# A two-layer encoder trunk on one core: the seams between a down projection and the next up projection reordered, six pairs begun in them instead of four

## The chip, the cores and the metric

The kernel runs on one core of one Trainium2 chip, as one launch. The metric is the device time of an execution in microseconds (us). The engines are called PE (matrix products and transposes), ACT (activations, copies, also a DMA queue), DVE (vector operations) and SP (a DMA queue); a thing "on PE" is an instruction in that engine's own queue.

## What is computed

The reference is a trunk of two layers over x of 1024 rows (tokens) by 1024 columns. Layer 0 mixes by a short gated convolution, layer 1 by attention over shared keys and values. Both are followed by a squared-ReLU MLP, and each of these four blocks is wrapped in the same way:

```python
h = modulate(rmsnorm(x, norm_g[l, 0]), sh_m, sc_m)
y = short_conv_mixer(h, ...) if l < N_A else mla_mixer(h, ...)
x = x + g_m[:, None, :] * rmsnorm(y, norm_g[l, 1])
h = modulate(rmsnorm(x, norm_g[l, 2]), sh_f, sc_f)
y = jnp.square(jax.nn.relu(h @ mlp_up_w[l])) @ mlp_down_w[l]
x = x + g_f[:, None, :] * rmsnorm(y, norm_g[l, 3])
```

So at the end of every block a product y is complete row by row, y is normalised and added to x, x is normalised again, scaled and shifted, and the result h is what the next block's first product takes. Between the two products lie two norms, a transposition and a split, for all 1024 rows. That stretch is called a seam here.

## The kernel before

**Numbers.** Every f32 factor is split into a high and a low part ("split": ACT writes the high part, DVE subtracts it for the low part; `split_w`, line 162), and a product is three matmuls (`mm`, line 158). One matmul is 128 by 128 by 512.

**Pairs.** The up projections (`mlp_up`, line 1051, and `all_pairs`, line 480) take the weight columns in pairs of 128, 16 pairs, and compute a pair against both halves of h (512 rows each) with seven instead of eight block products, in the manner of Strassen and Winograd. The operands on the side of h are quarters called "11", "21", "22" and the sums t1 to t4. "11" and "21" need only the first half of h (rows 0 to 511, y tiles 0 to 3); the others need the second half too. A product (`prod`, line 472) is twelve matmuls. A pair is "begun" when its products with "11" and "21" have been made ahead; the other five follow later. `AHEAD` (line 36) says how many pairs are begun in the seam. For a begun pair the later sums are taken by DVE (line 513), for the others by copies on ACT (line 511) and further adds.

**The seam** is written out by hand in the class `Seam` (line 258). The last round of the down projection (`down`, line 742) computes y in eight tiles of 128 rows; each is 24 matmuls in one of two wide PSUM tiles ("big"). After each tile t, `Seam.tile` (line 288) does this:

- DVE adds the tile from PSUM to y[t] (line 299);
- `back` (line 278) runs the splits left over from the last turn;
- `squares` (line 242): ACT squares y[t], sums the row and takes the root;
- `flush` (line 282): ACT normalises the tile before, y[t-1] <- x[t-1] times the reciprocal root (line 285);
- from t = 5 on, `front` (line 272) runs two steps of the first half: per step four transposes of y[0..3] on PE into a "tp" PSUM tile, of which there are two, and one eviction on ACT with scale and shift (lines 360 and 361; in the seam of layer 0's MLP lines 420 and 422). Its back, two operations on DVE (371 and 372, or 426 and 427), makes the split;
- DVE scales y[t] by its root and gain gmb (line 305) and adds it to x (line 306); the ACT queue stores x; ACT squares x[t], which the next flush uses.

Eight steps make the first half (`steps0`): six in tiles 5 to 7, the last two behind the seam's first product.

**Order.** `pinned` (line 101) chains every instruction issued in its block to the one before on the same engine, for all engines but SP. Inside such a block the order on an engine is the order of the program. Instructions outside, such as the matmuls of the next tile, are placed by the compiler's scheduler, which can put them ahead of a pinned instruction that it takes to be not ready.

**After the last tile** there are two forms. Seams one and three (behind the convolution's and the attention's output product) go to `first_pairs` (line 576): first(i) is the product of pair i with "11" and a copy of it on ACT (586); second(i) is the product with "21", added to the same PSUM bank, and its ReLU (590). Between them stand the turns of the second half: four steps (`steps1`), each of eight transposes and two evictions into a raw buffer (`front1`, 374) and a back (`back1`, 387) of five splits: five copies on ACT (382), eight subtractions on DVE (385 and 392 to 399). Pair 0's weight sums (`pair_sums`, 456) stand there too, and the five products that need the second half end it. Weights of pairs 0 to 2 are split before the seam; pair 3's come through the buffer "acc". Seam two (behind layer 0's MLP) goes to `first_block` (line 556): eight rounds of nine matmuls, with the second half turned from round 4 on.

**Buffers.** Raw buffers (line 91) are four and hold x tiles, weight blocks and turned quarters; row buffers (line 97) are eight and hold the eight y tiles, later the pairs' results; "acc" and "gmb" (in `ad`) are one each; split weights of a pair half have three.

**The last phase** is layer 1's down projection: the same `tile`, without the second norm, and `finish` (line 314) for its tile 7, in two halves.

Of the kernel before, what the change touches and what calls it, by code (L numbers as in the profile page):

```python
# [8 lines left out]
F32 = mybir.dt.float32  # L9
# [8 lines left out]
P = 128  # L18
D = 1024
# [13 lines left out]
SM = 1.0 / math.sqrt(NOPE + ROPE)  # L33
MASKED = -(2.0 ** 127)
SLOTS = 6
AHEAD = 4
ROWS = 4
LAG = 2
PAIRS = (D_FF // P - ROWS) // 2
# [10 lines left out]
def trunk_kernel(ctx: ExitStack, tc: tile.TileContext, x, c, ada_w, ada_b, norm_g, conv_in_w, conv_w,  # L50
# [31 lines left out]
    def mm_ps():  # L82
        return ps.tile([P, HALF], F32, tag="mm", name=nm("mm"))
# [166 lines left out]
    def rroot(rt):  # L250
        rs = small()
        nc.vector.reciprocal(rs, rt)
        return rs
# [4 lines left out]
    class Seam:  # L258
# [29 lines left out]
        def tile(self, t, p_, steps):  # L288
            y = self.ys[t]
            if t == 0:  # L290
                self.load(0)
                self.load(1)
            self.load(t + 2)
            xr = self.xr[t]
            if self.last and t == NT - 1:
                self.finish(t, y, xr, p_)
                return
            with pinned():
                nc.vector.tensor_tensor(y, y, p_, op=ALU.add)  # L299
                self.back()  # L300
                ss = squares(self.nx, y)
                self.flush()
                if t >= 5:
                    self.front(steps, 2)
                nc.vector.scalar_tensor_tensor(y, y, rroot(ss), self.gmb, op0=ALU.mult, op1=ALU.mult)  # L305
                nc.vector.tensor_tensor(xr, xr, y, op=ALU.add)  # L306
                nc.scalar.dma_start(self.xdst[t * P:(t + 1) * P, :], xr)
                if not self.last:
                    self.rest = (y, xr, squares(self.nx, xr))

        def finish(self, t, y, xr, p_):

# [240 lines left out]
    def first_block(seam, steps0, steps1, ws, h):  # L556

        ps_ = [mm_ps(), mm_ps(), big_ps()[:, :HALF]]
        for k in range(KD):
            with pinned():  # L560
                for p_, w in zip(ps_, ws):
                    mm(p_, (w[0][:, k, :], w[1][:, k, :]), (h[0][:, k, :], h[1][:, k, :]), k == 0, k == KD - 1)
                if k == 0:
                    seam.back()
                    seam.front(steps0, 2)
                    seam.flush()
                elif k == 1:
                    seam.back()
                elif k >= 4:
                    seam.back()  # L570
                    seam.front(steps1, 2)
        with pinned():
            seam.back()
        return ps_

    def first_pairs(seam, steps0, steps1, up, wmat, ws, ops):

        banks(True)
        tiles = [mm_ps(), mm_ps(), bank_ps(), bank_ps()]
        ca = [row_tile() for _ in range(AHEAD)]  # L580
        late = ad.tile([P, D], F32, tag="acc", name=nm("w"), bufs=1).rearrange("p (k m) -> p k m", k=KD)
        ld(late, wmat[:, 2 * (AHEAD - 1) * P:(2 * AHEAD - 1) * P].rearrange("(k p) m -> p k m", p=P))

        def first(i):
            prod(tiles[i], (ws[i], 0, "11"), ops)
            nc.scalar.activation(ca[i][:, HALF:], tiles[i], AF.Copy)  # L586

        def second(i):
            prod(tiles[i], (ws[i], 4, "21"), ops, False)
            nc.scalar.activation(ca[i][:, :HALF], tiles[i], AF.Relu)  # L590

        a, b = load_pair(wmat, 0)
        with pinned():
            first(0)
            seam.back()
            seam.front(steps0, 2)
            first(1)
            seam.back()
            seam.flush()
            second(0)  # L600
            ws.append(up_split(up, late))
            sums = pair_sums(up, a, b)
            next(sums)
            second(1)
            next(sums)
            seam.front(steps1, 1)
            rest = next(sums)
            first(2)
            seam.front(steps1, 1)
            seam.backs.pop(0)()  # L610
            second(2)
            rest.update(next(sums))
            first(3)
            seam.front(steps1, 1)
            seam.backs.pop(0)()
            out_ = {6: mm_ps(), 5: mm_ps(), 3: bank_ps(), 7: bank_ps(), 4: bank_ps()}
            for kk in range(4):
                for j in (5, 6, 4, 3, 7):
                    prod(out_[j], rest[j], ops, kks=[kk])
                if kk == 0:  # L620
                    second(3)
                    seam.front(steps1, 1)
                if kk < 2:
                    seam.backs.pop(0)()
            p1, cb = ca[0][:, HALF:], row_tile()
            c21, c22 = halves(cb)
            nc.vector.tensor_tensor(c21, p1, out_[6], op=ALU.add)
            nc.vector.tensor_tensor(c22, c21, out_[5], op=ALU.add)
            nc.vector.tensor_tensor(c21, c21, out_[4], op=ALU.add)
            nc.vector.tensor_tensor(p1, c22, out_[3], op=ALU.add)  # L630
            nc.vector.tensor_tensor(c22, c22, out_[7], op=ALU.add)
            nc.vector.tensor_tensor(c21, c21, out_[7], op=ALU.add)
# [396 lines left out]
    def down_phase(slots, sizes, wd, src_fn, g, xsrc, xdst, next_w, key, ys=None, pairs=True):  # L1029
# [6 lines left out]
        if pairs:  # L1036
# [1 line left out]
            hs = {n: as_quarter(slots[i]) for n, i in zip(names, (2, 3, 0, 1, 4, 5))}  # L1038
            hs["t4"] = {}
            steps0, steps1 = quarter_steps(ys, key, hs)  # L1040
            wcols = [next_w[:, 2 * i * P:(2 * i + 1) * P] for i in range(AHEAD - 1)]
        else:
            hs = [as_h(slots, H0), as_h(slots, H1)]
            steps0, steps1 = h_steps(tp, ys, 0, key, hs[0]), h_steps(tp, ys, 1, key, hs[1])
# [468 lines left out]
```

## Time and profile before

| | |
|---|---|
| median of 3 timed runs | 2180.91 us (2180.79 to 2181.0) |
| the profiled execution | 2184.31 us |
| its span, first to last instruction | 2182.5 us |
| mean granted clock of PE | 0.992 |
| busy: PE, DVE, ACT | 2091.3, 1518.8, 1065.7 us |
| DVE's add of tile 7, seams one, two, three | 389.86, 1047.39, 1534.77 us |

A line of the timeline gives the start and duration in us, the engine and source line, the operation, output <- input by the program's names, shapes and the count of instructions merged into it; in brackets the idle time of the engine ahead of it and what ended that. `L160` is the helper `mm`, so its lines are told apart by the names of tiles: "one", "mm" and "big" are PSUM tiles, "uphi" and "uplo" split weights, "slot" and "q" the operands made of h. A line of the waits gives the total, the number and the longest.

### The profile page before, as it was taken

Reading aid. Unit: us, or ns where it says so; the run is one execution under the profiler, and the core shown is the slowest. Engines: PE = TensorE matmul, PEld = TensorE weight load, DVE = VectorE, ACT = ScalarE, POOL = GpSimd, SP = SyncE. Lnnn points to the kernel's source line nnn. Section 1 sums busy time; section 2 is a strip of 40 time slices with the busy share of each in tenths; the row PEclk is TensorE's granted clock in tenths of the full one; section 3 lists DMA queues with packets and bytes.
Section 4 is the critical chain, followed back from the end, with each engine's and each line's share of the span. In section 5 each row is a group of like instructions: output and inputs, shape, how many; then the busy total and the mean of one; then the engine's idle time right before and its main releaser. Section 6 shows DMA issues by size and latency. Waiting matters only on the chain.

```text
span 2182.5 us, 25285 instructions
## 1 busy us (share of the span) xinstructions
PE 2091.3 (96%) x9654; PEld 1716.8 (79%) x9654; DVE 1518.8 (70%) x2009; ACT 1065.7 (49%) x1515; POOL 4.0 (0%) x8
## 2 busy tenths in 40 slices
PE   4999999899999999999899999999899999999998
PEld 3788878678888778888777888878678888788887
DVE  6877776876665578956788776665866665458556
ACT  4533354744454433344665555564744454444342
POOL 0000000000000000000000000000000000000000
PEclk9999999999999999999999999999999999999999
DMA  7444463256543987445224231053245553853243
GB/s 225 125 133 141 137 211 134 78 164 212 169 159 107 323 273 262 155 146 173 86 65 121 70 113 44 25 163 122 77 158 185 184 179 113 312 199 129 97 145 135
DMA packets 240255, 329.90 MB, mean 151 GB/s; under 512 B 18597, under 2 KB 141826, under 8 KB 240134
## 3 DMA queue, kind: packets, MB, share of 16 engines
q1 hardware_dynamic: 202248, 247.52, 36.2%
q10 hardware_dynamic: 37886, 80.77, 9.8%
q8 instruction: 76, 1.25, 0.2%
q14 instruction: 45, 0.37, 0.1%
HBM read 247.50 MB, written 80.74 MB: 150 GB/s over the span
## 4 chain that ended last, share of the span: by engine, by line
PE 73%; DVE 13%; ACT 6%; DMA 5%; issue 2%; ACTq 0%; SPq 0%; DVEq 0%
PE one L160 37%; PE mm L160 19%; PE tp L160 7%; PE big L160 4%; DMA raw<-in_ada_w_dram 3%; PE big L1306 2%; ACT junk L245 2%; DVE y L305 2%; DVE raw L306 2%; DVE acc L185 1%; PE tp L1332 1%; DVE y L299 1%; DVE av L847 1%; DMA raw<-ha 1%; DVE small L1309 1%
## 5 line engine op out<-in xcount | busy, mean ns | idle before, releaser
L160 PE MATMUL one<-slot,uphi 128*128 128x512 f32 x1224 | 377.8, 390 | 0.0
L160 PE MATMUL big<-slot 128*128 128x512 f32 x1152 | 268.0, 392 | 1.0 <-ACT y L770 0.6
L160 PEld LDWEIGHTS one<-slot,uphi 128*128 128x128 f32 x1224 | 230.6, 188 | 48.1 <-issue 0.5
L160 PEld LDWEIGHTS big<-slot 128*128 128x128 f32 x1152 | 216.0, 188 | 46.7 <-ACT y L770 1.4
L164 DVE TENSOR_TENSOR uplo<-raw,uphi 128x1024 fp32r<-128x1024 f32 x127 | 153.0, 1221 | 137.1 <-ACT uphi L163 137.1
L160 PE MATMUL one<-slot,uplo 128*128 128x512 f32 x612 | 240.8, 393 | 6.7 <-ACT y L586 2.3
L160 PE MATMUL one<-ring,ring 128*128 128x512 f32 x1008 | 232.3, 391 | 6.5 <-DVE ring L164 6.5
L163 ACT ACTIVATE ring<-w 128x1024 fp32r<-128x1024 f32 x98 | 103.8, 1059 | 261.4 <-PE tp L160 131.6
L160 PEld LDWEIGHTS one<-ring,ring 128*128 128x128 f32 x1008 | 188.2, 188 | 49.4 <-ACT ring L163 5.5
L163 ACT ACTIVATE uphi<-raw 128x1024 fp32r<-128x1024 f32 x127 | 134.5, 1061 | 129.5 <-PE one L160 89.1
L164 DVE TENSOR_TENSOR ring<-w,ring 128x1024 fp32r<-128x1024 f32 x98 | 119.8, 1222 | 107.5 <-ACT ring L163 107.4
L160 PE MATMUL mm<-slot,uphi 128*128 128x512 f32 x520 | 165.0, 398 | 9.7 <-DVE slot L385 9.3
L160 PE MATMUL mm<-ring,ring 128*128 128x512 f32 x672 | 162.4, 390 | 0.0
L160 PE MATMUL tp<-ring,ring 128*128 128x512 f32 x672 | 161.8, 389 | 0.0
L185 DVE SCALAR_TENSOR_TENSOR acc<-raw,csil,acc 128x1024 f32<-128x1024 f32 x88 | 112.8, 1282 | 49.8 <-DMA raw<-in_ada_w_dram 47.6
L160 PEld LDWEIGHTS mm<-ring,ring 128*128 128x128 f32 x672 | 125.7, 188 | 27.1 <-DVE ring L164 0.6
L160 PEld LDWEIGHTS tp<-ring,ring 128*128 128x128 f32 x672 | 126.2, 188 | 26.2
L160 PEld LDWEIGHTS one<-slot,uplo 128*128 128x128 f32 x612 | 115.3, 188 | 34.2 <-ACT y L511 3.3
L164 DVE TENSOR_TENSOR ring<-raw,ring 128x1024 fp32r<-128x1024 f32 x98 | 119.5, 1219 | 18.1 <-ACT ring L163 18.1
L160 PEld LDWEIGHTS mm<-slot,uphi 128*128 128x128 f32 x520 | 97.7, 190 | 33.2 <-DVE slot L385 10.8
L511 ACT ACTIVATE y<-one 128x512 f32<-128x512 f32 x66 | 39.0, 591 | 170.7 <-PE one L160 83.8
L160 PE MATMUL one<-slot,s 128*128 128x512 f32 x468 | 114.2, 393 | 0.7 <-DVE s L164 0.7
(262 smaller groups left out, 3473.3 us busy)
## 6 DMA issues: line engine op xcount, KB each, us to landing
ha<-y ACTq DMA_DIRECT2D x196, 256.0 KB, 3.9
raw<-ha SPq DMA_DIRECT2D x98, 512.0 KB, 4.0
raw<-in_ada_w_dram SPq DMA_DIRECT2D x80, 512.0 KB, 4.4
raw<-in_mlp_up_w_dram SPq DMA_DIRECT2D x70, 512.0 KB, 4.3
w<-in_mlp_down_w_dram SPq DMA_DIRECT2D x56, 512.0 KB, 5.9
raw<-hd SPq DMA_DIRECT2D x24, 512.0 KB, 4.5
xs<-raw ACTq DMA_DIRECT2D x24, 512.0 KB, 3.1
raw<-xs SPq DMA_DIRECT2D x24, 512.0 KB, 3.4
```

The lines of the kernel that those rows point to most:

```text
L160: nc.tensor.matmul(out_, lhs[a], rhs[b], start=first and i == 0, stop=last and i == 2, skip_group_check=more)
L163: nc.scalar.activation(hi, src, AF.Copy)
L164: nc.vector.tensor_tensor(lo, src, hi.bitcast(F32), op=ALU.subtract)
L185: nc.vector.scalar_tensor_tensor(acc, raw, s, acc, op0=ALU.mult, op1=ALU.add)
L245: nc.scalar.activation(junk, src, AF.Square, accum_out=ss)
L299: nc.vector.tensor_tensor(y, y, p_, op=ALU.add)
L305: nc.vector.scalar_tensor_tensor(y, y, rroot(ss), self.gmb, op0=ALU.mult, op1=ALU.mult)
L306: nc.vector.tensor_tensor(xr, xr, y, op=ALU.add)
L511: nc.scalar.activation(dst, x_, AF.Copy)
L847: nc.vector.scalar_tensor_tensor(acc, raw[:, i, :], csil[:, i:i + 1], acc, op0=ALU.mult, op1=ALU.add)
L1306: nc.tensor.matmul(o_, a, m_, start=j == 0, stop=j == 4 and b * HALF + w < n)
L1309: nc.vector.tensor_reduce(mx, sp[:, :n], AX.X, ALU.max, negate=True)
```

## The change

In `Seam.tile` the first half is turned from t = 4 on, so that tiles 4, 5, 6 and the last hold its eight steps. The last tile of a seam has an order of its own, `closing`: gmb is multiplied by y[7] while ACT squares it, the scaling and the add to x become one operation behind the root, ACT squares x at once, and then come the DMA, the splits left over and the last two steps of the first half. In the last phase tiles 1 to 6 multiply by gmb ahead of the root too, into the y tile of the tile before.

`AHEAD` is six. `first_pairs` begins six pairs, uses all four one-bank PSUM tiles for them, takes row buffers one at a time, and loads the weights of pairs 3, 4 and 5 one behind the other through "acc". The loads of pair 0's blocks stand behind the four turns. The turns stand in other places, and the back of the last one behind the first round of the five products. `first_block` loses its two turns of the first half.

```diff
--- before.py
+++ after.py
@@ -33,7 +33,7 @@
 SM = 1.0 / math.sqrt(NOPE + ROPE)
 MASKED = -(2.0 ** 127)
 SLOTS = 6
-AHEAD = 4
+AHEAD = 6
 ROWS = 4
 LAG = 2
 PAIRS = (D_FF // P - ROWS) // 2
@@ -295,21 +295,39 @@
             if self.last and t == NT - 1:
                 self.finish(t, y, xr, p_)
                 return
+            if t == NT - 1:
+                self.closing(t, y, xr, p_, steps)
+                return
             with pinned():
                 nc.vector.tensor_tensor(y, y, p_, op=ALU.add)
                 self.back()
                 ss = squares(self.nx, y)
                 self.flush()
-                if t >= 5:
+                if t >= 4:
                     self.front(steps, 2)
-                nc.vector.scalar_tensor_tensor(y, y, rroot(ss), self.gmb, op0=ALU.mult, op1=ALU.mult)
-                nc.vector.tensor_tensor(xr, xr, y, op=ALU.add)
+                if self.last and t:
+                    z = self.ys[t - 1]
+                    nc.vector.tensor_tensor(z, y, self.gmb, op=ALU.mult)
+                    nc.vector.scalar_tensor_tensor(xr, z, rroot(ss), xr, op0=ALU.mult, op1=ALU.add)
+                else:
+                    nc.vector.scalar_tensor_tensor(y, y, rroot(ss), self.gmb, op0=ALU.mult, op1=ALU.mult)
+                    nc.vector.tensor_tensor(xr, xr, y, op=ALU.add)
                 nc.scalar.dma_start(self.xdst[t * P:(t + 1) * P, :], xr)
                 if not self.last:
                     self.rest = (y, xr, squares(self.nx, xr))
 
-
-
+        def closing(self, t, y, xr, p_, steps):
+
+            with pinned():
+                nc.vector.tensor_tensor(y, y, p_, op=ALU.add)
+                ss = squares(self.nx, y)
+                nc.vector.tensor_tensor(self.gmb, self.gmb, y, op=ALU.mult)
+                self.flush()
+                nc.vector.scalar_tensor_tensor(xr, self.gmb, rroot(ss), xr, op0=ALU.mult, op1=ALU.add)
+                self.rest = (y, xr, squares(self.nx, xr))
+                nc.scalar.dma_start(self.xdst[t * P:(t + 1) * P, :], xr)
+                self.back()
+                self.front(steps, 2)
 
         def finish(self, t, y, xr, p_):
 
@@ -561,10 +579,7 @@
                 for p_, w in zip(ps_, ws):
                     mm(p_, (w[0][:, k, :], w[1][:, k, :]), (h[0][:, k, :], h[1][:, k, :]), k == 0, k == KD - 1)
                 if k == 0:
-                    seam.back()
-                    seam.front(steps0, 2)
                     seam.flush()
-                elif k == 1:
                     seam.back()
                 elif k >= 4:
                     seam.back()
@@ -576,52 +591,70 @@
     def first_pairs(seam, steps0, steps1, up, wmat, ws, ops):
 
         banks(True)
-        tiles = [mm_ps(), mm_ps(), bank_ps(), bank_ps()]
-        ca = [row_tile() for _ in range(AHEAD)]
-        late = ad.tile([P, D], F32, tag="acc", name=nm("w"), bufs=1).rearrange("p (k m) -> p k m", k=KD)
-        ld(late, wmat[:, 2 * (AHEAD - 1) * P:(2 * AHEAD - 1) * P].rearrange("(k p) m -> p k m", p=P))
+        tiles = [mm_ps(), mm_ps()] + [bank_ps() for _ in range(AHEAD - 2)]
+        ca = []
+
+        def late(i):
+            w = ad.tile([P, D], F32, tag="acc", name=nm("w"), bufs=1).rearrange("p (k m) -> p k m", k=KD)
+            ld(w, wmat[:, 2 * i * P:(2 * i + 1) * P].rearrange("(k p) m -> p k m", p=P))
+            return w
+
+        w = late(3)
 
         def first(i):
             prod(tiles[i], (ws[i], 0, "11"), ops)
+            ca.append(row_tile())
             nc.scalar.activation(ca[i][:, HALF:], tiles[i], AF.Copy)
 
         def second(i):
             prod(tiles[i], (ws[i], 4, "21"), ops, False)
             nc.scalar.activation(ca[i][:, :HALF], tiles[i], AF.Relu)
 
-        a, b = load_pair(wmat, 0)
+        def turn():
+            seam.front(steps1, 1)
+
+        def parts():
+            seam.backs.pop(0)()
+
         with pinned():
             first(0)
+            seam.flush()
             seam.back()
-            seam.front(steps0, 2)
             first(1)
-            seam.back()
-            seam.flush()
+            first(2)
+            turn()
             second(0)
-            ws.append(up_split(up, late))
+            parts()
+            ws.append(up_split(up, w))
+            second(1)
+            turn()
+            second(2)
+            w = late(4)
+            parts()
+            first(3)
+            ws.append(up_split(up, w))
+            second(3)
+            turn()
+            turn()
+            w = late(5)
+            a, b = load_pair(wmat, 0)
+            first(4)
+            parts()
+            ws.append(up_split(up, w))
+            second(4)
             sums = pair_sums(up, a, b)
             next(sums)
-            second(1)
+            first(5)
             next(sums)
-            seam.front(steps1, 1)
+            second(5)
             rest = next(sums)
-            first(2)
-            seam.front(steps1, 1)
-            seam.backs.pop(0)()
-            second(2)
             rest.update(next(sums))
-            first(3)
-            seam.front(steps1, 1)
-            seam.backs.pop(0)()
             out_ = {6: mm_ps(), 5: mm_ps(), 3: bank_ps(), 7: bank_ps(), 4: bank_ps()}
             for kk in range(4):
                 for j in (5, 6, 4, 3, 7):
                     prod(out_[j], rest[j], ops, kks=[kk])
                 if kk == 0:
-                    second(3)
-                    seam.front(steps1, 1)
-                if kk < 2:
-                    seam.backs.pop(0)()
+                    parts()
             p1, cb = ca[0][:, HALF:], row_tile()
             c21, c22 = halves(cb)
             nc.vector.tensor_tensor(c21, p1, out_[6], op=ALU.add)
@@ -1038,7 +1071,7 @@
             hs = {n: as_quarter(slots[i]) for n, i in zip(names, (2, 3, 0, 1, 4, 5))}
             hs["t4"] = {}
             steps0, steps1 = quarter_steps(ys, key, hs)
-            wcols = [next_w[:, 2 * i * P:(2 * i + 1) * P] for i in range(AHEAD - 1)]
+            wcols = [next_w[:, 2 * i * P:(2 * i + 1) * P] for i in range(3)]
         else:
             hs = [as_h(slots, H0), as_h(slots, H1)]
             steps0, steps1 = h_steps(tp, ys, 0, key, hs[0]), h_steps(tp, ys, 1, key, hs[1])
```

## Prediction

> **What bounds the kernel now.** Page part 1 first, then the waits of PE alone, longest first (total, times, longest one).
>
> ```profile
> PE 2091.3 (96%) x9654; PEld 1716.8 (79%) x9654; DVE 1518.8 (70%) x2009; ACT 1065.7 (49%) x1515; POOL 4.0 (0%) x8
> PE mm L160 <- DVE slot L385: 9.3, 4, 3.2
> PE tp L360 <- ACT q L361: 5.6, 4, 2.2
> PE tp L420 <- ACT tt L422: 4.4, 2, 3.4
> PE one L160 <- ACT y L586: 2.3, 2, 1.1
> ```
>
> PE is busy for 96% of the 2182.5 us span, so only its idle time can be won. These four waits, 21.6 us, all stand in the three seams. Lines 360 and 420 turn h, 385 splits its second half, 586 empties a begun pair. About 1% of the span is to be had here, plus what the clock loses behind such waits and the chain after the last matmul.
>
> Next the timeline of PE through the first seam, with two windows behind it; a window's row gives its length, then each engine's busy time, and PEclk, DMA share and GB/s last.
>
> ```profile
> 375.27 0.49 PE L360 MATMUL tp<-cs,y 128*128 128x128 f32 x3
> 379.97 0.71 PE L360 MATMUL tp<-cs,y 128*128 128x128 f32 x5
> 389.15 1.32 PE L360 MATMUL tp<-cs,y 128*128 128x128 f32 x8 [0.97 <-ACT q L361]
> 404.62 1.03 PE L360 MATMUL tp<-cs,y 128*128 128x128 f32 x8
> 405.41 0.48 PE L160 MATMUL one<-slot,uplo 128*128 128x512 f32 x1
> 437.87 1.22 PE L160 MATMUL mm<-slot,uphi 128*128 128x512 f32 x2 [3.25 <-DVE slot L385]
> 443.82 2.92 PE L160 MATMUL one<-slot,s 128*128 128x512 f32 x12
> 446.58 0.39 PE L160 MATMUL one<-slot,uplo 128*128 128x512 f32 x1
> 452.96 0.50 PE L160 MATMUL one<-slot,uplo 128*128 128x512 f32 x1 [0.78 <-DVE y L513]
> ...
> 433.47:436.88 3.41, 0.50 (x1) 0.19 (x1) 3.41 (x6) 1.46 (x4) 0.00 (x0) 0.98 0.01 3
> 436.88:440.29 3.41, 2.42 (x6) 1.94 (x7) 2.74 (x5) 0.39 (x1) 0.00 (x0) 0.50 0.09 23
> ```
>
> A product (12 matmuls) costs 446.58 - 443.82 = 2.75 us, a turn of eight transposes 405.41 - 404.62 = 0.8. The five products of pair 0 end at 443.82, where pair 1 begins, with 0.8 more lost at 452.96. Tile 7's matmuls end at 389.15 - 0.97 = 388.2. Two things matter beyond the waits. After a window in which PE worked 0.50 of 3.41 us its granted clock was 0.50. And the eight transposes of tile 5's front stand as three, then five 4.7 us later, between tile 6's matmuls: the order on PE was fixed for a normalisation of y[3] that ends then.
>
> **The change, part by part.**
>
> **1. First half turned a tile sooner (t >= 4).** The front that stood in tile 5 moves to tile 4, behind the flush that normalises y[3]. All of it, transposes, two evictions on ACT and two splits on DVE, needs y[3].
>
> ```profile
> 375.02 1.14 ACT L285 ACTIVATE y<-raw,small 128x1024 f32<-128x1024 f32 x1
> 377.92 0.33 ACTq L307 DMA_DIRECT2D xs<-raw  x1
> 378.29 1.06 ACT L245 ACTIVATE junk<-raw 128x1024 bf16<-128x1024 f32 x1 [2.14 <-DVE raw L306]
> 388.34 1.43 ACT L361 ACTIVATE q<-tp,v,v 128x512 f32<-128x512 f32 x2
> ...
> 1519.93 1.14 ACT L285 ACTIVATE y<-raw,small 128x1024 f32<-128x1024 f32 x1
> 1523.61 0.71 PE L360 MATMUL tp<-cs,y 128*128 128x128 f32 x5
> ...
> 1032.55 1.14 ACT L285 ACTIVATE y<-raw,small 128x1024 f32<-128x1024 f32 x1
> 1035.02 0.71 PE L420 MATMUL tp<-cs,y 128*128 128x128 f32 x5
> ```
>
> ACT normalises y[3] at 375.02 to 376.16 and today goes on to the squares at 378.29. In the new order two evictions stand between. The transposes of y[3] can't be placed earlier in PE's order than the place where the five stand now, since the same normalisation decides; PE comes to it at 379.97. So ACT, whose order is pinned, stands until 380.3; two evictions (0.66 apart) and the DMA's issue (0.33) follow, and the squares begin at 382.0, **3.7 us late**. DVE's next tile waits for them, and the loop DVE-ACT has no slack: tiles follow at 389.86 - 383.83 = 6.03 us (rows in part 2), while PE needs 5.5 for 24 matmuls. So the whole end of the seam comes 3.7 later. The same sum, squares 3.27 behind the start of the normalisation today and 2.03 behind PE's place then, gives a hold of 2.4 in seam three and 1.2 in seam two. Bounds: 0 (PE's order changes) to 3.7.
>
> **2. Closing: last tile's norms first.**
>
> ```profile
> 383.83 1.21 DVE L299 TENSOR_TENSOR y<-y,big 128x1024 f32<-128x1024 f32 x1
> 389.86 1.21 DVE L299 TENSOR_TENSOR y<-y,big 128x1024 f32<-128x1024 f32 x1
> 394.74 1.22 DVE L306 TENSOR_TENSOR raw<-raw,y 128x1024 f32<-128x1024 f32 x1
> 396.37 1.06 ACT L245 ACTIVATE junk<-raw 128x1024 bf16<-128x1024 f32 x1 [0.58 <-DVE slot L371]
> ```
>
> gmb*y moves beside ACT's squares, so after the root one DVE operation is left instead of two: the squares of x go from 396.37 to 394.76, 1.6 sooner. They end at 396.3; DMA issue (0.3), two evictions (1.3), the first copy (0.5) and the normalisation itself (1.1) follow, and y[7] is ready at 399.5, without the hold. The four splits that stood ahead now run behind, hidden by first(0) to first(2).
>
> **3. Six pairs in the seam, without the hold.** Prices:
>
> ```profile
> L164 DVE TENSOR_TENSOR uplo<-raw,uphi 128x1024 fp32r<-128x1024 f32 x127 | 153.0, 1221 | 137.1 <-ACT uphi L163 137.1
> 410.18 0.58 ACT L586 ACTIVATE y<-one 128x512 f32<-128x512 f32 x1
> 412.85 0.69 DVE L385 TENSOR_TENSOR slot<-raw,slot 128x512 fp32r<-128x512 f32 x1
> 416.71 0.69 DVE L385 TENSOR_TENSOR q<-sums,q 128x512 fp32r<-128x512 f32 x1
> ```
>
> A back of the second half costs 417.40 - 412.85 = 4.55 from its first split. Closing's turn needs the two PSUM tiles that the evictions at 388.34 free (389.1 and 389.8), so first(0) starts at F = 390.2. In us from F: three firsts end at 8.25; y[7] is ready at 9.3, turn 0 ends at 9.9 (PE waits 1.1); second(0) 12.65, second(1) 15.4, turn 1 16.2, second(2) 18.95. first(3) needs ws[3], split behind back 0: 19.6 to 22.35 (wait 0.65). **second(3) adds to the bank that ACT must first copy, and that copy stands behind back 1's splits: 24.1 to 26.85 (1.8).** Two turns in a row share two PSUM tiles: 29.2 (0.75). first(4) 31.95; copy; second(4) 32.6 to 35.4 (0.7). **first(5) needs ws[5], whose split stands behind all of back 2, which begins after the copy: 32.5 for the copy's end, 0.6 for the first split on ACT, 4.55, 1.2: 38.85 to 41.6 (3.5).** second(5) 45.0 (0.65). The five products take 13.65, with 1.25 and 1.55 for the split of s2 and t3: F + 61.5 = 451.7. Waits: 12 us, so the two extra pairs don't fill the seam; they bring copies with nothing between.
>
> Today's kernel reaches the same amount of work at 443.82 + 4 x 2.75 (pairs 4 and 5) + 0.8 = 455.6. So without the hold each of seams one and three ends **3.8** (rounded) sooner; with it, 0.1 and 1.4.
>
> **The clock.** With the hold PE stands about 3.3 us ahead of first(0) in seam one (tile 7 ends near 389.4, its 388.2 and eight transposes more, some with short waits; the eviction it needs ends at 388.34 + 3.7 + 0.7), and 3.5 at first(5). The window of 0.50 us work above cost the next windows half their clock. I take 1.5 a seam (a window of 3.41 us at half is 1.7), from 0 to 3.4. [...]
>
> **4. Seam two.**
>
> ```profile
> 1045.87 1.43 ACT L422 ACTIVATE tt<-tp,v,v 128x512 f32<-128x512 f32 x2
> 1046.68 1.46 PE L420 MATMUL tp<-cs,y 128*128 128x128 f32 x8 [3.40 <-ACT tt L422]
> 1062.08 1.04 PE L420 MATMUL tp<-cs,y 128*128 128x128 f32 x8
> ```
>
> Without the hold the turn of closing ends at 1047.75, five rounds of nine matmuls (2.05 each) and today's slow window (1.7) follow: the first turn of the second half at 1059.7 instead of 1062.08, 2.4 sooner. With the hold of 1.2 it starts from 1049.0 and loses 1.15 at half clock: 1060.4, **1.7** sooner.
>
> **5. Last phase.**
>
> ```profile
> 2173.92 1.23 DVE L306 TENSOR_TENSOR raw<-raw,y 128x1024 f32<-128x1024 f32 x1
> 2175.07 1.28 DVE L321 TENSOR_TENSOR y<-y,big 128x512 f32<-128x512 f32 x2
> ```
>
> Tile 6 keeps DVE until 2175.1, so tile 7's first half, long out of PE, is added with the second. With gmb*y ahead of the root DVE is free 1.2 sooner, the first add runs before the last matmul: **0.8** (0.6 for the add, the rest where the products with gmb no longer start late).
>
> **6. At nothing.** Pairs 4 and 5 leave their evictions to DVE (L513) as pairs 1 to 3 do; two products behind each take cover it, and without that cover it is some 0.8 each, the wait at 452.96. Background work begins two pairs later and has its ten tasks in pairs 6 to 15. The second load through acc waits for ws[3]'s split (F + 19.6), lands 4.3 later and is used at 24; the third and pair 0's two blocks queue on SP behind ws[4]'s split at 26.5 and have over 9 us.
>
> ```profile
> raw<-in_mlp_up_w_dram SPq DMA_DIRECT2D x70, 512.0 KB, 4.3
> 417.31 1.22 DVE L164 TENSOR_TENSOR uplo<-raw,uphi 128x1024 fp32r<-128x1024 f32 x1
> 418.55 0.37 SPq L115 DMA_DIRECT2D raw<-in_mlp_up_w_dram  x1
> ```
>
> **Sum.** Seam one 0.1 - 1.5, seam two 1.7, seam three 1.4 - 1.5, end 0.8: 1.0 us sooner. The profiled execution took 2184.31 (span 2182.5 and 1.8 around it), so 2183.3; the median of the timed runs stands 3.4 below it, which gives **2179.9**.
>
> **Rivals.**
>
> **No hold.** If PE turns y[3] as soon as it is ready, the seams bring 3.8, 2.4 and 3.8, the end 0.8: 10.8, or 7.8 with half clock after first(5): 2173.1 (2170.1 at best). For it: ACT's 2.14 us idle at 378.29 is just the room for two evictions. Against: three, 19 matmuls, five, the same in all three seams.
>
> **Slower: pair 1's second block comes late.** Four raw buffers now hold four turned quarters ahead of pair 0's blocks. If the fourth load goes into the buffer of the last quarter, it starts at F + 55 (all in this rival 3.7 later with the hold), lands 4.3 later, and sums and splits (5.5) bring s2 at F + 64.8, 3.3 after PE is ready, in seams one and three: 1.0 - 6.6, 2186.5. It decides if the buffer is freed after F + 51.7; pair 0's second block goes free at F + 47.5. Against it: at 418.55 the load took the buffer just released at 418.53, so the first free one is used.
>
> **The change doesn't do what it says** is the forecast itself: turned sooner in the program, at the same place on PE.
>
> **Chances.** Forecast 0.6, no hold 0.22, slower rival 0.15, else 0.03. Around the forecast the clock (0 to 3.4 a seam) and the waits of part 3 (1 us a seam) spread 4 us either way. Range 2171.5 to 2187.5: no hold without its best fifth, the slower rival just in. A measurement tells about 0.2% (4.4 us) from no change. Faster by that: most of no hold (0.2) and a seventh of the forecast (0.09); slower: the rival and a tenth of the forecast. Faster 0.29, same 0.5, slower 0.21.
>
> **What would show it.** Right: ACT idle 2 to 4 us ahead of an eviction (L361) in tile 4, ended by PE, and squares near 382 in seam one; second(3), second(4), second(5) each waiting for a copy; first(5) for a split. Wrong: tile 4's eviction directly behind the flush, or pair 1 waiting for a DMA.

## The result, and the profile after

The changed kernel takes 2209.6 us (median of 4 runs, 2205.92 to 2211.44), the kernel before, beside it, 2180.95 (2180.79 to 2181.2): 1.0129 times as long, 95% interval 1.0116 to 1.0142. The forecast was 1 us sooner; it came out 29 later, outside the range. The profiled execution took 2209.86 us, its span is 2208.1, the mean granted clock 0.990.

Busy times and PE's waits in the page and the waits view of the changed kernel (total, times, longest):

```profile
PE 2098.3 (95%) x9654; PEld 1719.9 (78%) x9654; DVE 1523.2 (69%) x2017; ACT 1060.4 (48%) x1507; POOL 4.0 (0%) x8
PE one L160 <- DVE y L531: 13.6, 6, 3.9
PE one L160 <- DVE uplo L164: 10.2, 6, 3.2
PE tp L378 <- ACT q L379: 6.5, 2, 3.2
PE one L160 <- ACT y L607: 5.7, 6, 1.5
PE one L160 <- DVE s L164: 5.1, 5, 1.3
```

The same 9654 matmuls take PE 7 us more busy time (2098.3 against 2091.3), most of it slower clock (mean granted 0.990 against 0.992); the other engines' work is what it was. The longest entry is new: line 531 (513 before) is DVE's take of a begun pair's product out of PSUM. Six times PE waited for it.

PE's timeline through seam one of the changed kernel, rows with a wait:

```profile
389.42 1.97 PE L378 MATMUL tp<-cs,y 128*128 128x128 f32 x8 [3.22 <-ACT q L379]
410.68 0.50 PE L160 MATMUL one<-slot,uplo 128*128 128x512 f32 x1 [0.60 <-DVE uplo L164]
415.23 0.50 PE L160 MATMUL one<-slot,uplo 128*128 128x512 f32 x1 [1.49 <-ACT y L607]
419.61 1.32 PE L378 MATMUL tp<-cs,y 128*128 128x128 f32 x8 [0.48 <-ACT raw L379]
424.36 0.50 PE L160 MATMUL one<-slot,uplo 128*128 128x512 f32 x1 [0.69 <-ACT y L607]
430.60 0.79 PE L160 MATMUL one<-slot,uplo 128*128 128x512 f32 x1 [3.23 <-DVE uplo L164]
436.77 0.50 PE L160 MATMUL one<-slot,uplo 128*128 128x512 f32 x1 [0.69 <-ACT y L607]
441.72 0.98 PE L160 MATMUL mm<-slot,s 128*128 128x512 f32 x3 [1.25 <-DVE s L164]
444.68 0.50 PE L160 MATMUL one<-slot,uplo 128*128 128x512 f32 x1 [1.28 <-DVE uplo L164]
457.42 3.04 PE L160 MATMUL one<-slot,s 128*128 128x512 f32 x12 [0.88 <-DVE s L164]
467.39 0.50 PE L160 MATMUL one<-slot,uplo 128*128 128x512 f32 x1 [1.50 <-DVE y L531]
482.58 3.04 PE L160 MATMUL one<-slot,s 128*128 128x512 f32 x12 [1.27 <-DVE s L164]
500.39 0.50 PE L160 MATMUL one<-slot,uplo 128*128 128x512 f32 x1 [3.87 <-DVE y L531]
517.54 0.50 PE L160 MATMUL one<-slot,uplo 128*128 128x512 f32 x1 [1.63 <-DVE y L531]
```

The first nine rows are the seam, 12.9 us of waits; from 457.42 on stand pairs 1 to 5, which wait 9.15 us in five places where the kernel before waits 0.78 in one. Seam three shows nearly the same.

Where the time arose, by one landmark, DVE's add of tile 7 in each seam of the changed kernel (389.86, 1047.39 and 1534.77 before):

```profile
390.14 1.21 DVE L322 TENSOR_TENSOR y<-y,big 128x1024 f32<-128x1024 f32 x1
1062.15 1.21 DVE L322 TENSOR_TENSOR y<-y,big 128x1024 f32<-128x1024 f32 x1
1549.29 1.21 DVE L322 TENSOR_TENSOR y<-y,big 128x1024 f32<-128x1024 f32 x1
```

The changed kernel is later by 0.3, 14.8 and 14.5 us there, and by 25.6 at the end. Seam two's stretch (1062.15 to 1549.29) costs nothing; the two stretches that begin with `first_pairs` cost it all. Within the first, pair 1 starts at 457.42, where the forecast's reckoning for the kernel before gave 455.6 for the same work. The changed execution was 2.8 us ahead when it came to the seam (the same matmul stands at 290.25 and at 293.08), so the seam itself, with the hold ahead of it, lost about 4.6, and the stretch from pair 1 to the add of seam two 13.0 (14.8 less 1.8).

### The profile page after: what moved, and what is told of

Its sections match the earlier page's. It is cut to its first block, busy times and chain, and to the rows that moved or that the text cites. A ratio compares the mean times of both kernels' runs of the same rounds, so it can differ in the third digit from the quotient of the medians.

```text
span 2208.1 us, 25297 instructions
## 1 busy us (share of the span) xinstructions
PE 2098.3 (95%) x9654; PEld 1719.9 (78%) x9654; DVE 1523.2 (69%) x2017; ACT 1060.4 (48%) x1507; POOL 4.0 (0%) x8
## 3 DMA queue, kind: packets, MB, share of 16 engines
q8 instruction: 76, 1.25, 0.2%
## 4 chain that ended last, share of the span: by engine, by line
PE 76%; DVE 11%; DMA 6%; ACT 4%; issue 2%; SPq 0%; ACTq 0%; DVEq 0%
PE one L160 35%; PE mm L160 18%; PE big L160 11%; PE tp L160 7%; DMA raw<-in_ada_w_dram 2%; PE big L1339 2%; DMA raw<-in_mlp_up_w_dram 2%; DVE acc L185 1%; PE tp L1365 1%; DVE uplo L164 1%; DVE small L1342 1%; ACT uphi L163 1%; PE tp L438 1%; DMA aw<-in_ada_w_dram 1%; DVE slot L403 1%
## 5 line engine op out<-in xcount | busy, mean ns | idle before, releaser
L160 PE MATMUL one<-slot,uphi 128*128 128x512 f32 x1256 | 391.9, 393 | 0.0
L160 PE MATMUL one<-slot,uplo 128*128 128x512 f32 x628 | 250.7, 399 | 31.6 <-DVE y L531 13.6
L160 PEld LDWEIGHTS one<-slot,uphi 128*128 128x128 f32 x1256 | 238.7, 190 | 49.7 <-issue 0.5
L164 DVE TENSOR_TENSOR uplo<-raw,uphi 128x1024 fp32r<-128x1024 f32 x123 | 148.4, 1221 | 133.0 <-ACT uphi L163 132.9
L160 PE MATMUL mm<-slot,uphi 128*128 128x512 f32 x488 | 154.5, 398 | 0.0
L160 PEld LDWEIGHTS one<-slot,s 128*128 128x128 f32 x468 | 88.2, 189 | 25.4 <-DVE s L164 6.9
```

The lines of the kernel that those rows point to most:

```text
L160: nc.tensor.matmul(out_, lhs[a], rhs[b], start=first and i == 0, stop=last and i == 2, skip_group_check=more)
L164: nc.vector.tensor_tensor(lo, src, hi.bitcast(F32), op=ALU.subtract)
```

## The experiments

Three theories were set against each other. **Begun pairs**: pairs 1 to 5, with five products instead of seven, use weights faster than the buffers let DVE and ACT prepare them. **Late load**: pair 0's weight blocks now stand behind the turns, so that all later blocks are late. **Hold**: turning at t = 4 delays the whole seam.

### Four pairs in the new order

```diff
-AHEAD = 6
+AHEAD = 4
...
-            first(4)
...
-            second(4)
...
-            first(5)
...
-            second(5)
```

> The changed kernel (2209.6 us) with four pairs begun instead of six, the rest of the change kept, the loads of pair 0 behind the four turns too. Begun-pairs theory (pairs 1 to 5, with five products each, outrun the buffers of their weights and lose some 9 us behind each of seams one and three): the waits behind the seam fall to 2 us or less, 2188 to 2197 us, part of it given back because the seam is less filled. Late-load theory (pair 0's blocks behind the turns make every later block late, however many pairs are begun): pairs 1 to 3 still lose 5 us or more a seam, 2200 us or more. Hold theory (ACT waiting for tile 4's transposes is the main loss): no change beyond 3 us, 2206 to 2213.

Measured: 2197.43 us (2196.77 to 2199.99), 1.0073 times before (1.0056 to 1.009): 0.4 above what the begun-pairs theory expected, and below what the late-load theory did. PE's timeline of this kernel:

```profile
433.65 0.80 PE L160 MATMUL mm<-slot,uplo 128*128 128x512 f32 x1 [9.64 <-DVE uplo L164]
451.28 3.02 PE L160 MATMUL one<-slot,s 128*128 128x512 f32 x12 [0.71 <-DVE s L164]
461.03 0.50 PE L160 MATMUL one<-slot,uplo 128*128 128x512 f32 x1 [1.29 <-DVE y L531]
```

Behind the seam the waits fall from 9.15 to 2.0 us. The loads are still late: pair 1's two blocks are issued at 429.4 and 436.4 (428.8 and 442.3 in the changed kernel, 418.6 and 423.7 in the kernel before). With four pairs this lateness costs 1.2 us more than the 0.78 of before. What remains above before is mainly the 9.64: the back of the last two turns and the sums of pair 0, with no products left to cover them.

### The turn one tile later again

The two turns of the first half stand behind the first product again, in `first_block` too (not shown):

```diff
-                if t >= 4:
+                if t >= 5:
...
             first(0)
+            seam.front(steps0, 2)
             seam.flush()
             seam.back()
```

> The changed kernel with the first half turned from tile 5 on again, two of its steps left for behind the first product, as before the change. Hold theory: 4 us of ACT's wait go in seam one, 2.5 and 1.5 in three and two, and with them the most of the loss: 2199 us or less. Begun-pairs theory and late-load theory: the hold goes, a wait of PE for the last turn comes in its place, and the waits of pairs 1 to 5 stay as they are: 2203 to 2210 us.

Measured: 2219.3 us (2215.68 to 2221.47), 1.0168 (1.0152 to 1.0184). The wait of the last first-half turn falls from 3.22 to 0.97, but the first product then waits 3.23 for the splits of that turn, which closing puts last; the pairs behind wait as in the changed kernel. Taking the hold away brings nothing here: its wait only stands in another place. The kernel is slower still, by 9.7 us, which none of the theories expected; why was not found out.

### The tiles' part alone

The kernel before, its four pairs and their order, with t >= 4, `closing` and the new order of the last phase:

```diff
-                if t >= 5:
+                if t >= 4:
...
             first(0)
-            seam.back()
-            seam.front(steps0, 2)
-            first(1)
-            seam.back()
             seam.flush()
+            seam.back()
+            first(1)
             second(0)
```

> The kernel before (2180.9 us) with the tiles' part of the change alone: turned from tile 4 on, closing for the last tile, the last phase's new order; four pairs, loads and turns of the second half where they were. Begun-pairs and late-load theory: no loss behind the seams, the hold against closing's gain: 2176 to 2186 us. Hold theory: slower than before by 10 us or more, 2191 us or more. The end after the last matmul stays at the length of before, 7.9 us.

Measured: 2183.53 us (10 runs, 2181.01 to 2185.17), 1.0007 (0.9998 to 1.0016): no difference. Hold, closing and the last phase together come to zero, so the loss must lie in `first_pairs` and what follows it.

### Four buffers of split weights in the changed kernel

```diff
-tag="uphi", name=nm("uphi"), bufs=3
+tag="uphi", name=nm("uphi"), bufs=4
...
-tag="uplo", name=nm("uplo"), bufs=3
+tag="uplo", name=nm("uplo"), bufs=4
```

> The changed kernel with four buffers instead of three for the split weights of a pair half. Begun-pairs theory: ACT no longer waits up to 8.8 us for PE before it splits a block, raw buffers come free sooner, the waits of PE in pairs 1 to 5 fall from 9.2 us to 5 or less a seam: 2194 to 2204 us. Late-load and hold theory: within 3 us of the changed kernel, 2206 to 2213 us.

Measured: 2195.77 us (2192.3 to 2197.59), 1.006 (1.0044 to 1.0076). Behind seam one two waits are left of five:

```profile
457.83 4.44 PE L160 MATMUL one<-slot,s 128*128 128x512 f32 x12 [2.54 <-DVE s L164]
498.41 0.50 PE L160 MATMUL one<-slot,uplo 128*128 128x512 f32 x1 [0.76 <-DVE y L531]
```

3.3 us instead of 9.15, and 13.8 us of the 28.7 gone with one buffer more. How three buffers starve PE is to be read in the changed kernel's own timeline, ahead of the wait at 500.39:

```profile
488.38 1.06 ACT L163 ACTIVATE uphi<-raw 128x1024 fp32r<-128x1024 f32 x1 [8.78 <-PE one L160]
489.47 1.22 DVE L164 TENSOR_TENSOR uplo<-raw,uphi 128x1024 fp32r<-128x1024 f32 x1 [0.41 <-ACT uphi L163]
490.73 0.37 SPq L115 DMA_DIRECT2D raw<-in_mlp_up_w_dram  x1
496.11 0.69 DVE L477 TENSOR_TENSOR raw<-raw,raw 128x512 f32<-128x512 f32 x1 [3.74 <-DMA raw<-in_mlp_up_w_dram]
499.65 0.68 DVE L531 TENSOR_TENSOR y<-y,one 128x512 f32<-128x512 f32 x1
```

Read it downward. ACT stands 8.78 us before a split, until PE is done with a product: `all_pairs` runs a pair's products with t3 and t2 (blocks 3 and 4) inside the next pair, so both buffers of the old pair are held, and the third has the next pair's t2; its t3 has to wait. The raw block that t3 is made of stays full until the split ends (490.69), and only then, at 490.73, SP issues the load into it. DVE waits 3.74 us for that load, until 496.11, and then works without a gap on what stands ahead of the take that PE needs; the take starts at 499.65, PE has been idle since 496.52. PE starts 0.1 us after that take ends. With a fourth split buffer the first link is shorter, not gone: ACT still stands before such splits, 5.6 to 6.0 us, but the loads behind them are issued earlier.

### Pair 0's blocks loaded early again

```diff
+        a, b = load_pair(wmat, 0)
         with pinned():
             first(0)
...
             w = late(5)
-            a, b = load_pair(wmat, 0)
```

> The changed kernel with one line moved: the loads of pair 0's two weight blocks are issued ahead of first(0) again, as before the change, instead of behind the four turns. Late-load theory (the loss behind the seam comes from this place of the loads alone): the weights of pairs 1 to 5 come some 20 us sooner again, the waits for DVE's takes (L531) in pairs 1 to 5 of seams one and three fall from about 9 us each to about 1, the time to about 2194. Begun-pairs theory (pairs with five products use weights faster than four raw and three split buffers let DVE and ACT prepare them): pair 1's blocks can load only when pair 0's sums have freed their buffers, and those sums stand where they stood, so the waits stay within 2 us of 9 a seam; the two blocks hold two of four raw buffers during the turns, which adds 0 to 4 us a seam there: 2207 to 2218.

Measured: 2208.29 us (2206.7 to 2208.97), 1.0118 (1.0105 to 1.0132). The waits behind seam one are 0.65, 1.22, 1.19, 3.82 and 1.61, 8.5 in all: the place of this load is not the cause. Pair 1's blocks are still issued late (431.2 and 443.8), because pair 0's sums stand where they stood, so this run says nothing of their lateness; the run with five pairs and three buffers, below, does.

### Five pairs, four split buffers, the old order

The kernel before with one more pair, its weights through "acc" behind those of pair 3:

```diff
-AHEAD = 4
+AHEAD = 5
...
             seam.backs.pop(0)()
+            ws.append(up_split(up, w))
+            second(3)
+            first(4)
+            seam.front(steps1, 1)
+            seam.backs.pop(0)()
```

> The kernel before with five pairs begun instead of four and four buffers of split weights instead of three: the fifth pair's product with 11 stands between the third and fourth turn, its weights come through acc behind those of pair 3, pair 0's blocks stay ahead of the turns, and the tiles' part of the change is left out. If the loss of the change lies in the lead of the weights and not in begun pairs as such, the extra pair fills waits of 1.4, 1.2 and 3.3 us and their slow clock, and its cover is kept by the fourth split buffer: 2170 to 2177. If each further begun pair runs dry whatever the order (about 4.5 us each in the changed kernel for two more, per seam), it gives the gain back: 2180 to 2188.

The control, the kernel before with four split buffers alone:

> The kernel before with four buffers of split weights instead of three and nothing else: the control of the run with five pairs and of the changed kernel with four such buffers. Begun-pairs theory: with four begun pairs only one wait of 0.8 us a seam stands behind the seam, so the fourth buffer has nothing to win: 2179 to 2184, within 0.1% of before. If three buffers are short everywhere (all 32 pairs), it is faster by 5 us or more, and what the fourth buffer gave in the changed kernel (13.8 us) says little about the seams.

And five pairs with the tiles' part of the change added:

> The run with five pairs and four split buffers, with the tiles' part of the change added: first half turned from t = 4, the closing order, gmb times y ahead of the root in the last phase. Hold theory: the tiles' part alone is neutral (2183.5 beside 2182.0), so this is within 3 us of the run with five pairs. If the tiles' part gains only where more products follow the turn, it is 3 to 6 us faster than that run.

Measured: five pairs 2180.88 us (11 runs, 2179.64 to 2184.66), 0.9996 (0.9987 to 1.0005); the control 2179.87 (11 runs, 2176.34 to 2184.09), 0.999 (0.9981 to 0.9999); with the tiles' part 2182.62 (11 runs, 2179.91 to 2185.87), 1.0001 (0.9992 to 1.001). The fourth buffer gives the kernel before some 0.1%: its three are no bound with four begun pairs. The tiles' part is neutral a second time. In seam one the hoped gain of five pairs failed in one place:

```profile
422.08 0.80 PE L160 MATMUL one<-slot,uplo 128*128 128x512 f32 x1 [4.86 <-DVE uplo L164]
```

The weights of pair 4 had been issued at 401.82, but their split stood behind the eight subtractions of a back on DVE.

### Five pairs, the split ahead of the turn

```diff
             first(3)
+            ws.append(up_split(up, w))
             seam.front(steps1, 1)
             seam.backs.pop(0)()
-            ws.append(up_split(up, w))
             second(3)
```

> The run with five pairs and four split buffers, with one line moved: the split of pair 4's weights stands ahead of the third turn and its back instead of behind them. In that run PE stood once, 4.9 us ahead of first(4) in seam one, for this split, which DVE reached only behind the eight subtractions of back 1; the load had landed long before. Order theory (what the turns' backs have ahead of a weight split decides the seam): the wait falls under 0.5 us and the half clock behind it goes too, about 5 us a seam: 2168 to 2174. Rival (work on DVE is the bound and the wait only moves): back 1 is 1.2 us later and a round of the five products waits 3 us or more for it: 2177 to 2181.

Measured: **2167.96 us** (2166.48 to 2170.27), beside 2180.81 of before: 0.994 (0.9928 to 0.9952), the fastest of all versions. One line moved gave some 12 us over the run without it (0.994 against 0.9996 of before). PE's longest waits in seam one behind the second product, and two windows (length, then PE's busy time; PEclk third from last):

```profile
436.62 0.73 PE L160 MATMUL mm<-slot,uphi 128*128 128x512 f32 x2 [1.31 <-DVE slot L385]
449.20 0.50 PE L160 MATMUL one<-slot,uplo 128*128 128x512 f32 x1 [0.94 <-DVE y L513]
```

```profile
385.00:445.00 60.00, 54.93 (x259) 43.28 (x258) 53.46 (x83) 42.91 (x68) 0.96 (x1) 1.00 0.31 94
445.00:530.00 85.00, 84.06 (x371) 69.30 (x370) 64.30 (x86) 41.77 (x49) 0.00 (x0) 1.00 0.63 203
```

The same windows of the changed kernel:

```profile
385.00:445.00 60.00, 47.05 (x203) 36.31 (x202) 40.19 (x61) 39.02 (x64) 0.95 (x1) 0.91 0.25 76
445.00:530.00 85.00, 75.85 (x322) 60.75 (x321) 58.90 (x84) 34.97 (x40) 0.00 (x0) 0.98 0.48 157
```

In the same 145 us this run makes 630 matmuls and the changed kernel 525, and its granted clock stays at 1.00.

### The same with three split buffers

```diff
-tag="uphi", name=nm("uphi"), bufs=4
+tag="uphi", name=nm("uphi"), bufs=3
...
-tag="uplo", name=nm("uplo"), bufs=4
+tag="uplo", name=nm("uplo"), bufs=3
```

> The same kernel as the run with five pairs and the split first, with three buffers of split weights as before the change. Theory that begun pairs run dry by their number: the pairs behind the seam wait 2 to 4 us more a seam than with four buffers, total 4 to 8 us above that run. Theory that the changed kernel lost through the missing lead (pair 0's blocks behind the turns, so all later blocks late): here the blocks stand ahead of the turns, so the waits behind the seam stay near 1 us and the time within 2 us of that run.

Measured: 2190.49 us (2186.81 to 2192.55), 1.0038 (1.0025 to 1.0051), 22.5 us above the run with four, about three times what the begun-pairs theory expected. PE's timeline:

```profile
419.26 0.50 PE L160 MATMUL one<-slot,uplo 128*128 128x512 f32 x1 [2.41 <-DVE uplo L164]
452.15 0.50 PE L160 MATMUL one<-slot,uplo 128*128 128x512 f32 x1 [0.78 <-DVE y L513]
469.70 4.44 PE L160 MATMUL one<-slot,s 128*128 128x512 f32 x12 [3.65 <-DVE s L164]
486.65 0.50 PE L160 MATMUL one<-slot,uplo 128*128 128x512 f32 x1 [1.61 <-DVE y L513]
```

Here all loads are early, as in the kernel before, and still the pairs behind the seam wait 6.0 us. In both such seams and the pairs behind them PE waits 16.6 us longer than in the run with four, and its busy time is 6.8 us longer (2094.2 against 2087.4), much of it slower clock (mean granted 0.992 against 0.994). So late load falls, and begun pairs stand, though their price was set too low: the lead carries one pair, and the fifth begun pair is one too many for three buffers (in the seam too, at 419.26).

### Splits ahead of the backs in the changed kernel

With four split buffers, the splits of pairs 3 and 5 ahead of a back:

```diff
-            parts()
             ws.append(up_split(up, w))
+            parts()
```

> The changed kernel with four split buffers (2195.8 us), with two lines moved: the splits of the weights of pairs 3 and 5 stand ahead of a turn's back instead of behind it. The waits ahead of first(3) and first(5), 0.6 and 3.2 us, stood for these splits. Order theory: both go, the backs and the sums of pair 0 come 1.2 us later, so some of it returns at the five products; 2 to 4 us a seam with the clock: 2188 to 2192. Rival (PE's waits there follow from DVE's work as a whole): within 1.5 us of 2195.8.

Measured: 2193.78 us (2193.23 to 2196.72), 1.006 (1.0047 to 1.0073), 2 us below 2195.77; but each is 1.006 times the kernel before that ran beside it, so a gain is not shown. The waits of 0.6 and 3.2 for the splits are gone, but the copy of a begun pair (L607) now stands behind the split on ACT, and PE waits 4.37 for it at 416.77. What the changed order holds above the old one with four buffers, some 14 us, could not be won by this edit; which order of these parts would win it was not tried. A fifth raw buffer was not tried either.

## Why the prediction was wrong

**The step that failed is part 6, "At nothing".** It said that pairs 4 and 5 leave their takes to DVE as pairs 1 to 3 do, "two products behind each take cover it", "some 0.8 each" without. The cover is there only if DVE comes to the take, and DVE stood in its queue for weight blocks: 9.15 us in seam one, 9.0 in seam three, and a stretch at half clock behind the longest. That is about 10 us a seam, two thirds of the miss. The slower rival had looked at the raw buffers of pair 0 and at the second block of pair 1, and missed the three split buffers, which decide when a raw buffer is free. Four split buffers in the changed kernel (minus 13.8 us) and three in the run with five pairs (plus 22.5) show that they are the cause of these waits. By the runs that is about half of the loss: with four buffers 3.3 us of these waits are left behind seam one, and the changed kernel is still some 14 us slower than before. No run took that part away.

**The clock was sized wrong**, 1.5 us a seam. Windows of the changed kernel, cut where the granted clock changes:

```profile
385.54:388.95 3.41, 0.66 (x5) 0.34 (x3) 3.31 (x7) 3.23 (x8) 0.00 (x0) 1.00 0.24 96
388.95:392.36 3.41, 2.94 (x11) 2.75 (x12) 3.34 (x4) 2.79 (x6) 0.00 (x0) 0.50 0.38 154
426.50:429.91 3.41, 0.87 (x4) 0.38 (x2) 3.41 (x6) 2.50 (x4) 0.00 (x0) 1.00 0.00 1
429.91:433.32 3.41, 2.72 (x6) 2.15 (x7) 1.93 (x3) 0.00 (x0) 0.95 (x1) 0.50 0.55 156
433.32:436.73 3.41, 2.76 (x7) 1.65 (x5) 0.00 (x0) 0.61 (x2) 0.00 (x0) 0.50 0.00 0
494.77:498.18 3.41, 1.75 (x8) 1.13 (x6) 2.08 (x3) 0.59 (x1) 0.00 (x0) 1.00 0.73 267
498.18:501.59 3.41, 1.20 (x5) 1.02 (x6) 3.41 (x7) 0.63 (x1) 0.00 (x0) 1.00 0.41 154
501.59:505.00 3.41, 3.41 (x9) 2.65 (x9) 1.75 (x3) 0.00 (x0) 0.00 (x0) 0.50 0.43 132
```

The waits of 3.22, 3.23 and 3.87 us are each followed by a window at half clock, the one at 430 by two. PE's work in these windows takes nearly twice its time: busy throughout, it has 9 matmuls in the window from 501.59 on and 16 in the 3.41 us behind it, at 1.00. Taken as twice, up to 436.7 it loses half of 2.94 + 2.72 + 2.76, that is 4.2 us, and 1.7 more from 501.59 on. The forecast had named the first two places and priced less than one window for the two.

**The hand-run of the seam held.** Forecast against measured, in us: first(3) 0.65 and 0.60, second(3) 1.8 and 1.49, turn behind turn 0.75 and 0.48, second(4) 0.7 and 0.69, first(5) 3.5 and 3.23, second(5) 0.65 and 0.69, s2 1.25 and 1.25, t3 1.55 and 1.28. Only the wait ahead of turn 0 (1.1) did not come. (One sum is off by a little: 455.6 - 451.7 is 3.9, not 3.8.)

**The hold held too**, and so the rival without it falls. PE keeps the transposes of y[3] where they were, and ACT stands for them in tile 4:

```profile
366.79 0.38 PE L378 MATMUL tp<-cs,y 128*128 128x128 f32 x2
370.22 0.27 PE L378 MATMUL tp<-cs,y 128*128 128x128 f32 x1
376.93 0.71 PE L378 MATMUL tp<-cs,y 128*128 128x128 f32 x5
377.24 0.78 ACT L379 ACTIVATE q<-tp,v,v 128x512 f32<-128x512 f32 x1 [4.13 <-PE tp L378]
```

The price was 3.3 us ahead of the last turn; 3.22 came. So first(0) started as forecast, at 391.04: 390.2 + 3.7, less the 2.8 that this execution was ahead, is 391.1. But closing and the turn taken out of `first_pairs` gave it back, so that the tiles' part was neutral.

**Seam two.** From the add of tile 7 to the first turn of the second half it was 1062.08 - 1047.39 = 14.7 us, forecast 11.8 (1060.4, with the add 1.2 later); the turn stands at 1074.17, 12.0 behind the add. A window at half clock 37 us later (1098.92 to 1102.33, granted 0.50), which the kernel before doesn't have there, took about 1.7 back, half of its length.

**The last phase** brought nothing instead of 0.8. DVE was free in time, but the first half's add waited:

```profile
2200.59 1.28 DVE L339 TENSOR_TENSOR y<-y,big 128x512 f32<-128x512 f32 x2 [1.19 <-PE big L160]
```

Both halves start when PE has finished the tile, not when the first half is done; from there to the end of the span it is 7.5 us, as it was (7.4). That the add waits for the tile as a whole is what the row suggests; no run split the tile.

The terms add up in the main: two seams with 8.4 more waits behind them (9.15 less 0.78), 2.7 and 1.7 more lost to the clock and 1.1 less at turn 0 make 23.4 (seam one's figures, taken for both); seam two fell short by about 1.4, the end by 0.8: 25.6. The profiled execution was 26.6 above its forecast of 2183.3, and would have been some 29 without the 2.8 that it was ahead by when it came to seam one. So 3 to 4 us are not assigned; about 3 of the 13.0 between pair 1 and seam two's add are among them.

## What to carry to other kernels

Work begun early doesn't only fill a gap: it leaves a lighter remainder, and the buffers that feed the remainder must turn over faster. Before such a step is costed at nothing, follow one buffer round: who frees it, what that waits for, and what stands behind the waiting instruction on its engine: here DVE waited 3.74 us for a load, and the take that PE needed started 3.5 us after it. And a weight split is best put ahead of a long row of other splits on the same engine; with five pairs one line's place was worth some 12 us. In the changed kernel the same move showed no gain: a copy on ACT then stood behind the split, and PE waited 4.37 us for it. So the place has to be checked on every engine that the split uses.

## What the runs showed of the hardware

The granted clock fell also behind windows in which PE worked. In the profiles of the kernel before and of the changed kernel, from 60 us after the start on and without the last 13 us, a stretch at 0.50 lasts 3.41 us or twice that, and the stretches of a profile begin a whole number of 3.41 us apart: before at 283.15, 436.75, 1047.74, 1436.86 and 1580.22 (45, 224, 338 and 380 such windows behind the first), changed at 388.95, 429.91, 501.59, 1061.37, 1098.92, 1549.48, 1590.44 and 1658.71 (12, 33, 197, 208, 340, 352 and 372).

The windows of 3.41 us ahead of a fall, shown above, had 0.66, 0.87 and 1.20 us of PE's work in them, and the granted clock behind them was 0.50; the one with 1.75 in the same rows had 1.00 behind it. In these two profiles all eleven windows at full clock with 1.57 us or less of PE's work (0.50, 1.05 and 1.57 before, eight from 0.00 to 1.40 changed) were followed by a fall. Of those with 1.75 or more two were, both before: the one from 1433.45 on with 2.07 us, 12 matmuls with two transposes among them, and the one with 2.69 us below.

All ten waits of PE of 3.2 us or more in them (3.22 to 3.87) have a fall inside or at most 1.2 us behind. Waits of about 2 us differ: one of 2.01 us in the changed kernel, ended at 1098.22, lay in a single window (1095.51 to 1098.92, 1.40 us of work) and was followed by a fall; 2.05 and 2.25 us in the kernel before, ended at 1086.16 and 1534.06, lay across two windows each (2.24 and 2.54 us of work, 2.79 and 1.76) and were not. So with these three it was not the length of the wait that decided; what went with the fall was how the wait lay to the windows.

In the kernel before it fell even behind a window with 2.69 us of PE busy, most of whose matmuls (16 of 21) were one column wide, which no run tested alone:

```profile
279.88:283.29 3.41, 2.69 (x21) 2.47 (x20) 2.99 (x5) 2.04 (x3) 0.00 (x0) 0.98 0.27 35
283.29:286.70 3.41, 3.41 (x10) 2.64 (x9) 3.30 (x4) 1.14 (x2) 0.00 (x0) 0.52 0.93 348
```

The same stretch of the changed kernel kept its clock (1.00 from 276.47 to 290.11). That kernel was 1.4 us ahead when it came there (its matmuls of one column start at 278.38, those of the kernel before at 279.76) and 2.8 us ahead when it had passed. Such a window, up to 1.7 us (an estimate, half of 3.41), came in one of the two profiles and not in the other; whether it explains small differences that no edit made was not shown.
